# Rows that carry their expert's number, and activations in smaller steps

## The chip, the core and the metric

The kernel runs on one core of a Trainium2 chip. The core has a matrix engine (TensorE, PE in the trace), three engines for other arithmetic (VectorE = DVE, ScalarE = ACT, GpSimd = POOL), a queue engine (SyncE = SP) and 16 DMA engines. Each engine works through its own instructions in order; semaphores tie them together. The metric is the device time of one execution in microseconds, the median of several runs.

## The reference

One decoder block over 256 tokens of 1024 numbers: modulation by a conditioning vector (adaLN), two attention branches with gates, and an expert layer of 128 x 128 experts. The expert layer is the part that the change touches:

```python
q = (ht @ w_pq).reshape(T, PEER_HEADS, 2, PEER_HALF)          # 256 tokens, 8 heads
sub = jnp.einsum('thpc,hpnc->thpn', q, peer_keys)             # scores of 128 keys, twice a head
s_top, i_top = lax.top_k(sub, 16)
cand_s = s_top[:, :, 0, :, None] + s_top[:, :, 1, None, :]    # 16 x 16 sums
best_s, pos = lax.top_k(cand_s.reshape(T, 8, 256), 16)
expert = jnp.take_along_axis(cand_i, pos, axis=-1)            # 128 experts for each token
gate = jax.nn.softmax(best_s, axis=-1)
act = jax.nn.gelu(jnp.einsum('cd,ckd->ck', xc, peer_u[expert]))
out = jnp.einsum('ck,ckd->cd', gate * act, peer_v[expert])
```

## The kernel before

It computes the expert layer densely: every expert's activation for all 256 tokens, times a weight that is zero where the token did not choose the expert. Experts stand in 128 row blocks of 128: block `j` holds the experts 128 p + j, p being the partition. One block of `u` is a load of 512 KB on SP, a copy to a high half on ACT, the rest as a low half by a subtraction (`split`, L94) on DVE or GpSimd, and 24 matmuls on PE (eight chunks, three each: high x high, high x low, low x high). Blocks go in pairs; a pair ends in gelu on ACT and 256 KB of activations.

The stages in order, with the function that stands for each:

- attention, merge, and the query projection (`proj` of `w_pq`). The first five sixths of the adaLN rows come as `background` work in the attention (`ada`, two rows of 512 KB a time, called by `bg`), the last eight in the query projection (`ada_one`).
- search: for each half of the tokens, four groups of scores, each with `top16` on DVE, then the sums, `top16` again, and the selection: comparisons and products over 128x2048 bf16 (`eq`) on DVE, softmax, transposes on PE.
- grid: 64 steps of four tokens. DVE writes one-hot tables `E`, `A` and twice `B`, PE multiplies them (`grid_mm`, 16 matmuls), ACT copies the product to `G`, the weights of all blocks.
- ranking: from a count `used`, each of the 120 x 128 experts of blocks 0 to 119 is classed (first half of the tokens, both, second half, none) and gets a place `at_i`.
- put: the row of 256 weighted activations of each expert goes by an indirect DMA (scatter, issued on POOL) to its place in `w_rows` in memory. Blocks that were done before `G` was there had their activations spilled to `act_spill`; `put_rows` loads them back into one of four buffers `w`, DVE multiplies by `G`, POOL scatters. Blocks done after that are scattered straight from the tile `as`. Beside it, `sort_some` builds the inverse list, from place to expert, with one-hot tables `R`, `C`, `N` and 120 matmuls into `listed`; the end of it is the list `expert`.
- last stage: `w_rows` is read in order of the places, class by class; rows of one class need only one half of the tokens. Blocks 120 to 127 (`d`) take no places. For each 128 places the rows of `v` are gathered by an indirect DMA with the indices `expert[:, c]`, split, and multiplied into four accumulators.

What sets the order: the program is written out in one order, and each engine gets its instructions nearly in that order; a load is issued as soon as its buffer is free. How many blocks of `u` go beside the search and the grid is set by shares: `u_some(share)` collects shares and issues a whole pair, 48 matmuls, when they reach one. `PACE_R` and `PACE_G` divide the shares of the search and of the grid. Low halves are made by GpSimd (`split_by`) until the places are known, and by DVE from then on. Everything waits in order on its engine, so a multiplication that waits for its load holds the splits behind it.

Of the kernel before, what the change touches and what calls it, by code (L numbers as in the profile page):

```python
# [11 lines left out]
I32 = mybir.dt.int32  # L12
# [20 lines left out]
PACE_R = 3.8  # L33
PACE_G = 5.0
# [5 lines left out]
def kernel(  # L40
# [39 lines left out]
    w_rows = dpool.tile([NQ * P, T], F32, name="w_rows")  # L80
# [124 lines left out]
    background = [lambda t=t: ada(t) for t in range(16, 40, 2)]  # L205
# [384 lines left out]
    def upair(j, name):  # L590
        ps = pp.tile([P, 2, T], F32, tag="pp", name=f"pu{name}")
        for s in range(2):
            hi, lo = unit(u[j + s], f"u{j + s}")
            for k in range(NC8):
                mm3(ps[:, s], hi[:, k], lo[:, k], hh[:, k], hl[:, k], k == 0, k == NC8 - 1)
        return ps

    def u_spill(j):
        a = upool.tile([P, 2, T], F32, tag="a", bufs=2, name=f"as{j}")
        after, low[0] = low[0], split_by[0]  # L600
        nc.scalar.activation(a, upair(j, f"s{j}"), AF.Gelu_apprx_tanh)  # L601
        low[0] = after
        if places:
            nc.vector.tensor_mul(a, a, Gs[0][:, j : j + 2] if j < NQ else Gs[1][:, j - NQ : j - NQ + 2])  # L604
        if places and j < NQ:
            for s in range(2):
                put_row(a[:, s], j + s)
        else:
            nc.scalar.dma_start(act_spill[j // 2], a.rearrange("p a t -> p (a t)"))


    places, Gs, scatters = [], [], []
# [81 lines left out]
    for tt in range(2):  # L694
# [3 lines left out]
        for q in range(4):  # L698
# [169 lines left out]
    rc_i = npool.tile([P, 2, P], I32, name="rc_i")  # L868
    nc.vector.tensor_scalar(rc_i[:, 0], at_i, P - 1, None, op0=OP.bitwise_and)
    nc.vector.tensor_scalar(rc_i[:, 1], at_i, 7, None, op0=OP.logical_shift_right)  # L870
    rc = qpool.tile([P, 2, P], BF16, name="rc")
    nc.vector.tensor_copy(rc, rc_i)
    col = qpool.tile([P, P], BF16, name="col")
    nc.vector.tensor_copy(col, iota4[:, :, 0])
# [9 lines left out]
    listed = pn.tile([P, 2, NQ], F32, tag="n", name="listed")  # L884
    places.append(at_i)
    split_by[0] = nc.vector
    first_put = spilled[0]

    def sort_some(b):

        j4 = slice(4 * b, 4 * b + 4)
        R = spool.tile([P, P, 4], BF16, tag="R", name=f"R{b}")
        C = spool.tile([P, 2, NQ, 2], BF16, tag="C", name=f"C{b}")
        N = spool.tile([P, 2, 2, NQ, 2], BF16, tag="N", name=f"N{b}")
        pairs = lambda x: x[:, j4].rearrange("p (h i) -> p h i", h=2)[:, :, None, :].to_broadcast([P, 2, NQ, 2])
        nc.vector.tensor_tensor(R, rc[:, 0, None, j4].to_broadcast([P, P, 4]), iota4, op=OP.is_equal)
        nc.vector.tensor_tensor(
            C, pairs(rc[:, 1]), iota4[:, None, 0:NQ, 0:2].to_broadcast([P, 2, NQ, 2]), op=OP.is_equal
        )
        nc.scalar.activation(N[:, :, 0], C, AF.Copy, scale=row)  # L900
        nc.vector.tensor_tensor(N[:, :, 1], C, pairs(col), op=OP.mult)
        for i in range(4):
            j = 4 * b + i
            nc.tensor.matmul(listed, R[:, :, i], N[:, i // 2, :, :, i % 2], start=(j == 0), stop=(j == NQ - 1))
# [19 lines left out]
    for j in puts:  # L924
        put_rows(j)
# [235 lines left out]
```

## Time and profile before

| | us |
|---|---|
| median of 3 runs | 1123.38 (1122.06 to 1124.8) |
| profiled execution | 1127.95 |
| its span | 1126.2 |
| busy in the span: PE, DVE, ACT, POOL | 1007.6, 815.6, 556.0, 436.6 |

The span is the time between the first and the last instruction of the core; the profiled execution's own time is 1.75 us longer. "Busy" is the time in which an engine has an instruction in work; issuing a DMA from a queue is not counted, but POOL's work for an indirect DMA is. Matmuls are pipelined, so that the mean time of one in the trace is longer than the distance from one to the next.

### The profile page before, as it was taken

What the parts mean: (1) busy time and instruction counts of PE and PEld (TensorE: products, weight loads), DVE (VectorE), ACT (ScalarE), POOL (GpSimd) and SP (SyncE); (2) the same over time, 40 slices, a digit from 0 to 9 for tenths busy, and PEclk for the clock granted to TensorE, in tenths of its full rate; (3) what the DMA queues carried; (4) which work ended last, traced back from release to release, by engine and by line L of the source; (5) the groups of instructions that cost most, each with busy time, mean ns of one, the idle gap of its engine ahead of it and who ended that gap; (6) DMA issues with size and microseconds to landing.
All of it is one profiled execution on the core that took longest, in us unless ns stands there. A gap on an engine that the chain in (4) does not pass through costs nothing. (4 is left out here: it accounts for less than half of the span.)

```text
span 1126.2 us, 19893 instructions
## 1 busy us (share of the span) xinstructions
PE 1007.6 (89%) x7540; PEld 925.1 (82%) x7543; DVE 815.6 (72%) x1589; ACT 556.0 (49%) x779; POOL 436.6 (39%) x293
## 2 busy tenths in 40 slices
PE   7889999989989796888888988777999899999995
PEld 4879989988989696878888987766999688888884
DVE  7788877775579999888777565556764577767765
ACT  4495345654455354444444533333553466656652
POOL 0000000000186677333333377776644065666540
PEclk9999999998999898999999999998999999999998
DMA  9964575346764455233222577777867799999981
GB/s 344 368 237 148 183 256 212 132 154 235 270 216 169 159 187 189 67 108 109 94 94 95 191 241 248 253 255 263 265 216 269 271 306 307 312 317 303 324 282 39
DMA packets 90826, 244.65 MB, mean 217 GB/s; under 512 B 10977, under 2 KB 33121, under 8 KB 90594
## 3 DMA queue, kind: packets, MB, share of 16 engines
q1 hardware_dynamic: 63794, 162.24, 42.9%
q0 software_dynamic: 20592, 69.74, 17.3%
q10 hardware_dynamic: 6336, 11.31, 2.7%
q8 instruction: 61, 1.00, 0.4%
q14 instruction: 43, 0.35, 0.1%
HBM read 215.20 MB, written 28.05 MB: 216 GB/s over the span
## 5 line engine op out<-in xcount | busy, mean ns | idle before, releaser
L96 POOL TENSOR_TENSOR l_u<-r_u,h_u 128x1024 fp32r<-128x1024 f32 x66 | 170.3, 2595 | 457.4 <-ACT h_u L95 457.4
L101 PE MATMUL pus<-hh_n,l_u 128*128 128x256 f32 x1024 | 297.9, 291 | 25.6 <-DVE l_u L96 25.5
L99 PE MATMUL pus<-hh_n,h_u 128*128 128x256 f32 x1024 | 299.7, 293 | 1.0 <-ACT as L601 1.0
L100 PE MATMUL pus<-hl_n,h_u 128*128 128x256 f32 x1024 | 295.1, 288 | 0.0
L95 ACT ACTIVATE h_u<-r_u 128x1024 fp32r<-128x1024 f32 x128 | 135.5, 1060 | 224.7 <-DMA r_u<-in_u_dram 108.4
L101 PEld LDWEIGHTS pus<-hh_n,l_u 128*128 128x128 f32 x1024 | 201.1, 196 | 30.0 <-DVE l_u L96 29.9
L99 PEld LDWEIGHTS pus<-hh_n,h_u 128*128 128x128 f32 x1024 | 201.6, 197 | 1.4 <-ACT as L601 1.2
L100 PEld LDWEIGHTS pus<-hl_n,h_u 128*128 128x128 f32 x1024 | 200.9, 196 | 0.0
L96 DVE TENSOR_TENSOR l_v<-r_v,h_v 128x1024 fp32r<-128x1024 f32 x111 | 133.7, 1224 | 46.8 <-ACT h_v L95 42.8
L978 POOL DMA_INDIRECT r_v<-in_v_dram,expert x103 | 122.0, 1184 | 115.5 <-DVE l_v L96 90.4
L95 ACT ACTIVATE h_v<-r_v 128x1024 fp32r<-128x1024 f32 x111 | 116.7, 1054 | 45.6 <-PE acc L101 36.8
L818 DVE TENSOR_TENSOR B<-E,selT 128x768 bf16<-128x768 bf16 x128 | 96.1, 783 | 31.7 <-PE used L801 30.4
L615 POOL DMA_INDIRECT w_rows<-w,at_i x66 | 80.5, 1219 | 37.3 <-ACT N L900 11.3
L797 PE MATMUL pg<-B,A 128*128 128x128 bf16 x768 | 70.5, 228 | 26.2 <-DVE B L818 19.8
L96 DVE TENSOR_TENSOR l_u<-r_u,h_u 128x1024 fp32r<-128x1024 f32 x62 | 75.8, 1223 | 24.3 <-ACT h_u L95 24.1
L797 PEld LDWEIGHTS <-A 128*128 128x128 bf16 x768 | 61.2, 116 | 32.3 <-issue 20.7
L615 POOL DMA_INDIRECT w_rows<-as,at_i x54 | 63.7, 1179 | 45.5 <-DVE as L604 33.6
L100 PE MATMUL acc<-l_v,whb 128*128 128x512 f32 x200 | 78.7, 394 | 2.5 <-DVE l_v L96 2.5
L99 PE MATMUL acc<-h_v,whb 128*128 128x512 f32 x200 | 78.2, 392 | 0.5 <-PEq L1020 0.5
L101 PE MATMUL acc<-h_v,wlb 128*128 128x512 f32 x200 | 78.5, 393 | 0.1
L911 DVE TENSOR_TENSOR w<-w,G 128x256 f32<-128x256 f32 x66 | 27.9, 427 | 62.0 <-DMA w<-act_spill 61.6
L805 ACT ACTIVATE G<-pg 128x480 f32<-128x480 f32 x64 | 36.5, 570 | 62.6 <-PE pg L797 58.8
(370 smaller groups left out, 2338.3 us busy)
## 6 DMA issues: line engine op xcount, KB each, us to landing
r_u<-in_u_dram SPq DMA_DIRECT2D x128, 512.0 KB, 3.7
ada<-in_w_ada_dram SPq DMA_DIRECT2D x20, 1024.0 KB, 7.7
act_spill<-as ACTq DMA_DIRECT2D x37, 256.0 KB, 3.3
w<-act_spill SPq DMA_DIRECT2D x66, 128.0 KB, 3.1
r_g<-in_w_in_dram SPq DMA_DIRECT2D x16, 512.0 KB, 3.9
r_pq<-in_w_pq_dram SPq DMA_DIRECT2D x16, 512.0 KB, 5.8
ab<-w_rows SPq DMA_DIRECT2D x25, 256.0 KB, 5.9
r_first<-in_w_in_dram SPq DMA_DIRECT2D x8, 512.0 KB, 7.1
```

The source lines that it names most:

```text
L95: nc.scalar.activation(hi, src, AF.Copy)
L96: last_split[:] = [low[0].tensor_sub(lo, src, hi.bitcast(F32))]
L99: nc.tensor.matmul(ps, lh, rh, start=start, stop=False)
L100: nc.tensor.matmul(ps, lh, rl, start=False, stop=False)
L101: nc.tensor.matmul(ps, ll, rh, start=False, stop=stop)
L615: o = nc.gpsimd.indirect_dma_start(out=w_rows, out_offset=bass.IndirectOffsetOnAxis(ap=places[0][:, j : j + 1], axis=0), in_=w, in_offset= ...
L797: nc.tensor.matmul(ps[:, t], A[:, :, t], Bs[t // 2][:, x, :, t % 2], start=(x == 0), stop=(x == 2))
L805: nc.scalar.activation(g[:, :, 4 * b : 4 * b + 4], ps[:, :, q].rearrange("p t j -> p j t"), AF.Copy)
L818: nc.vector.tensor_tensor(B, E[:, None, :, 2 * q : 2 * q + 2].to_broadcast([P, 3, P, 2]), g, op=OP.mult)
L911: nc.vector.tensor_mul(w, w, G[:, j + s])
L978: nc.gpsimd.indirect_dma_start(out=raw, out_offset=None, in_=v, in_offset=bass.IndirectOffsetOnAxis(ap=expert[:, c : c + 1], axis=0))
```

## The change

- **The number in the row.** `w_rows` has 257 columns (`ROW`) instead of 256. Between the two halves of the tokens, at column 128, stands the number of the row's expert, 128 p + j, written by ACT into the tile before the scatter. So `sort_some`, `listed` and `expert` go. Tiles that are scattered get a gap: 128 columns, the number, 128 columns; the load from the spill is cut into two pieces of 128 columns. In the last stage the weights' load brings the number along (rows of one half: 129 columns, from one side or the other), and the gather of `v` takes its index from that tile.
- **Steps.** `u_steps` is a generator that gives the work on `u` in steps of one chunk, three matmuls; 16 steps are a pair. The load and split of a block are issued two blocks ahead of its matmuls.
- **Shares.** `PACE_R` 3.8 becomes 3.2 and `PACE_G` 5.0 becomes 3.3; one more pair goes before the transposes of each selection.
- **Splits.** GpSimd makes low halves only from the first group of scores up to the third of each half of the tokens; DVE makes the rest.
- **adaLN.** All rows come in the attention, four more pairs by `bg(2)`; `ada_one` goes.
- **Buffers.** `w` eight instead of four, loaded weights four instead of three, their halves four instead of two, and weights are loaded three items ahead instead of two.

```diff
-PACE_R = 3.8
-PACE_G = 5.0
+PACE_R = 3.2
+PACE_G = 3.3
+ROW = T + 1
-    background = [lambda t=t: ada(t) for t in range(16, 40, 2)]
+    background = [lambda t=t: ada(t) for t in range(16, 48, 2)]
...
-            bg()
+            bg(2)
...
+    def u_done(j, ps):
+        a = upool.tile([P, 2, ROW + 1], F32, tag="a", bufs=2, name=f"as{j}")
+        if places and j < NQ:
+            ah = a.rearrange("p s (h n) -> p s h n", h=2)[:, :, :, 0:P]
+            th = lambda x: x.rearrange("p s (h t) -> p s h t", h=2)
+            nc.scalar.activation(ah, th(ps), AF.Gelu_apprx_tanh)
+            nc.vector.tensor_mul(ah, ah, th(Gs[0][:, j : j + 2]))
+            nc.scalar.activation(a[:, :, P : P + 1].bitcast(I32), numbers[0][:, j : j + 2, None], AF.Copy)
+            for s in range(2):
+                put_row(a[:, s, 0:ROW], j + s)
...
+        make(0)
+        make(1)
+        for j in range(0, NJ, 2):
+            ps = pp.tile([P, 2, T], F32, tag="pp", name=f"pu{j}")
+            for s in range(2):
+                if j + s + 2 < NJ:
+                    make(j + s + 2)
+                hi, lo = ready.pop(0)
+                for k in range(NC8):
+                    mm3(ps[:, s], hi[:, k], lo[:, k], hh[:, k], hl[:, k], k == 0, k == NC8 - 1)
+                    if s == 0 or k < NC8 - 1:
+                        yield
+            u_done(j, ps)
+            done[0] = j + 2
+            yield
...
     def u_some(share):
-        spilled[1] += share
-        while spilled[1] >= 1.0 and spilled[0] < NJ:
-            u_spill(spilled[0])
-            spilled[0] += 2
-            spilled[1] -= 1.0
+        owed[0] += 2 * NC8 * share
+        while owed[0] >= 1.0:
+            owed[0] -= 1.0
+            next(steps, None)
...
-            for t in range(32 + 2 * b, 34 + 2 * b) if b >= 4 else ():
-                ada_one(t)
...
+            split_by[0] = nc.gpsimd if q < 3 else nc.vector
             u_some(4.0 / PACE_R)
...
+        u_some(1.0)
         ps = pr_.tile([P, 3, P], F32, tag="t", name=f"psel{tt}")
...
-            w = spool.tile([P, T], F32, tag="w", bufs=4, name=f"w{j + s}")
-            nc.sync.dma_start(w, act_spill[j // 2][:, T * s : T * s + T])
-            nc.vector.tensor_mul(w, w, G[:, j + s])
-            put_row(w, j + s)
+            w = spool.tile([P, ROW + 1], F32, tag="w", bufs=8, name=f"w{j + s}")
+            wh = w.rearrange("p (h n) -> p h n", h=2)[:, :, 0:P]
+            th = lambda x: x.rearrange("p (h t) -> p h t", h=2)
+            nc.sync.dma_start(wh, th(act_spill[j // 2][:, T * s : T * s + T]))
+            nc.vector.tensor_mul(wh, wh, th(G[:, j + s]))
+            nc.scalar.activation(w[:, P : P + 1].bitcast(I32), number[:, j + s : j + s + 1], AF.Copy)
+            put_row(w[:, 0:ROW], j + s)
...
+    for i in range(2 * left):
+        u_some(0.5)
+        while puts and n_puts - len(puts) < n_puts * (i + 1) / max(1, 2 * left - 6):
             put_rows(puts.pop(0))
...
-            out=raw, out_offset=None, in_=v, in_offset=bass.IndirectOffsetOnAxis(ap=expert[:, c : c + 1], axis=0)
+            out=raw, out_offset=None, in_=v, in_offset=bass.IndirectOffsetOnAxis(ap=no, axis=0)
```

How this moves instructions shows at three places. The first is DVE in the middle of the grid; `l_u` is a low half of `u`. Before:

```order
L811 TENSOR_TENSOR E_6816<-selT,iota_2860 128x512
L818 TENSOR_TENSOR B_0_6820<-E_6816,selT 128x768
L818 TENSOR_TENSOR B_1_6822<-E_6816,selT 128x768
L811 TENSOR_TENSOR A_6844<-selT,iota_2860 128x512
L811 TENSOR_TENSOR E_6843<-selT,iota_2860 128x512
```

And after:

```order
L830 TENSOR_TENSOR E_6943<-selT,iota_2888 128x512
L837 TENSOR_TENSOR B_0_6947<-E_6943,selT 128x768
L98 TENSOR_TENSOR l_u_6937<-r_u_6934,h_u_6936 128x1024
L830 TENSOR_TENSOR A_6944<-selT,iota_2888 128x512
L837 TENSOR_TENSOR B_1_6949<-E_6943,selT 128x768
```

The low halves, which stood on POOL in the grid, now stand between the one-hot tables on DVE.

The second is DVE in the put stage; `w` are the reloaded blocks, `as` a pair that is put straight. Before:

```order
L911 TENSOR_TENSOR w_8841<-w_8841,G 128x256
L911 TENSOR_TENSOR w_8845<-w_8845,G 128x256
L896 TENSOR_TENSOR R_8590<-rc,iota_2860 128x512
L901 TENSOR_TENSOR N_8592<-C_8591,col 128x2x240
L96 TENSOR_TENSOR l_u_8551<-r_u_8548,h_u_8550 128x1024
L604 TENSOR_TENSOR as_8346<-as_8346,G 128x512
L897 TENSOR_TENSOR C_8761<-rc,iota_2860 128x480
L911 TENSOR_TENSOR w_8849<-w_8849,G 128x256
```

And after:

```order
L98 TENSOR_TENSOR l_u_8963<-r_u_8960,h_u_8962 128x1024
L605 TENSOR_TENSOR as_8933<-as_8933,G 128x4x128
L909 TENSOR_TENSOR w_9036<-w_9036,G 128x2x128
L909 TENSOR_TENSOR w_9041<-w_9041,G 128x2x128
L98 TENSOR_TENSOR l_u_9003<-r_u_9000,h_u_9002 128x1024
L909 TENSOR_TENSOR w_9046<-w_9046,G 128x2x128
L909 TENSOR_TENSOR w_9051<-w_9051,G 128x2x128
L909 TENSOR_TENSOR w_9087<-w_9087,G 128x2x128
```

The one-hot tables are gone, and between two pairs of `u` stand about six multiplications of reloaded blocks instead of four.

The third is POOL where the put stage ends. Before, the gathers of `v` take their indices from the list:

```order
L615 DMA w_rows<-w_10235,at_i 15360x256
L615 DMA w_rows<-as_9215,at_i 15360x256 x2
L978 DMA r_v_10681<-in_v_dram,expert 128x1024
L978 DMA r_v_10687<-in_v_dram,expert 128x1024
L978 DMA r_v_10711<-in_v_dram,expert 128x1024
```

And after, from the loaded weights `a` (one half of the tokens) and `ab` (both):

```order
L591 DMA w_rows<-w_10086,at_i 15360x257
L976 DMA r_v_10482<-in_v_dram,a_10365 128x1024
L976 DMA r_v_10488<-in_v_dram,a_10365 128x1024
L976 DMA r_v_10512<-in_v_dram,a_10407 128x1024
L976 DMA r_v_10518<-in_v_dram,a_10407 128x1024
L976 DMA r_v_10542<-in_v_dram,ab_10449 128x1024
```

Each gather now stands behind the load of its own weights, and the last scatters are those of reloaded blocks, no longer of direct ones.

## Rows read from the trace of the kernel before

**Rows 1.** Busy time by stretch: from:to, length, busy (instructions) per engine, clock, DMA.

```profile
core 0: us, PE busy (x) PEld busy (x) DVE busy (x) ACT busy (x) POOL busy (x), PEclk, DMA share, GB/s
307.00:450.00 143.00, 120.39 (x955) 118.48 (x955) 129.58 (x465) 70.44 (x81) 102.73 (x40) 0.92 0.54 185
450.00:620.00 170.00, 143.75 (x1603) 137.69 (x1603) 135.68 (x250) 71.25 (x163) 60.52 (x24) 0.96 0.28 94
620.00:639.00 19.00, 19.00 (x167) 18.89 (x167) 9.75 (x29) 9.01 (x13) 4.85 (x2) 1.00 0.51 173
639.00:793.00 154.00, 121.97 (x925) 116.36 (x925) 91.91 (x172) 56.20 (x72) 111.12 (x96) 0.94 0.76 249
793.00:874.00 81.00, 80.65 (x673) 79.93 (x672) 51.31 (x71) 39.72 (x50) 39.94 (x30) 1.00 0.77 257
...
924.00:1092.00 168.00, 168.00 (x743) 139.12 (x742) 119.90 (x127) 105.98 (x127) 99.01 (x84) 1.00 0.91 310
```

**Rows 2.** Waits of PE: waited for what, us in total, times, longest.

```profile
PE pus L101 <- DVE l_u L96: 25.5, 20, 3.4
PE pg L797 <- DVE B L818: 19.8, 12, 1.8
PE psel L769 <- DVE sel L758: 16.7, 2, 9.0
```

**Rows 3.** Tiles eq and B (min/median/max ns), and GpSimd's splits (busy us, mean ns).

```profile
L754 DVE TENSOR_TENSOR eq<-rb,ranks x4: 1209/3434/3446, 355.2 to 433.2; 128x2048 bf16<-128x2048 bf16 x4
L755 DVE TENSOR_TENSOR eq<-eq,at x4: 3370/3445/3449, 356.5 to 439.4; 128x2048 bf16<-128x2048 bf16 x4
...
L818 DVE TENSOR_TENSOR B<-E,selT x128: 546/556/2789, 386.4 to 617.3; 128x768 bf16<-128x768 bf16 x128
...
L96 POOL TENSOR_TENSOR l_u<-r_u,h_u 128x1024 fp32r<-128x1024 f32 x66 | 170.3, 2595 | 457.4 <-ACT h_u L95 457.4
```

**Rows 4.** One grid step on DVE, then on PE: start us, length us, instruction.

```profile
480.74 0.42 DVE L811 TENSOR_TENSOR A<-selT,iota 128x512 bf16<-128x512 bf16 x1
...
481.53 1.03 DVE L818 TENSOR_TENSOR B<-E,selT 128x768 bf16<-128x768 bf16 x2
482.47 0.42 DVE L811 TENSOR_TENSOR A<-selT,iota 128x512 bf16<-128x512 bf16 x1
...
480.41 0.37 PE L797 MATMUL pg<-B,A 128*128 128x128 bf16 x3 [0.35 <-ACT Gd L805]
...
481.36 0.36 PE L101 MATMUL pus<-hh_n,l_u 128*128 128x256 f32 x1
```

**Rows 5.** Groups of instructions: busy us, mean ns, idle time before and its releaser.

```profile
L615 POOL DMA_INDIRECT w_rows<-as,at_i x54 | 63.7, 1179 | 45.5 <-DVE as L604 33.6
...
L911 DVE TENSOR_TENSOR w<-w,G 128x256 f32<-128x256 f32 x66 | 27.9, 427 | 62.0 <-DMA w<-act_spill 61.6
```

**Rows 6.** Scatters on POOL in order of time, and a split on DVE beside one.

```profile
707.49 0.96 POOL L615 DMA_INDIRECT w_rows<-as,at_i  x1 [0.30 <-DVE C L897]
...
847.99 1.89 POOL L615 DMA_INDIRECT w_rows<-as,at_i  x1 [0.31 <-issue]
...
847.82 1.23 DVE L96 TENSOR_TENSOR l_u<-r_u,h_u 128x1024 fp32r<-128x1024 f32 x1 [1.36 <-ACT h_u L95]
```

**Rows 7.** The tile w_rows (min/median/max ns, first and last start), and the gathers.

```profile
L615 POOL DMA_INDIRECT w_rows<-w,at_i x66: 955/962/2024, 639.4 to 795.3; - x66
L615 POOL DMA_INDIRECT w_rows<-as,at_i x54: 954/960/2012, 650.3 to 854.1; - x54
...
L978 POOL DMA_INDIRECT r_v<-in_v_dram,expert x103 | 122.0, 1184 | 115.5 <-DVE l_v L96 90.4
```

**Rows 8.** DMA queues and times to landing, 672 to 784 us; last, 924 to 1090.

```profile
q1 hardware_dynamic: 10536, 19.12, 55.5%
q0 software_dynamic: 3408, 9.31, 21.4%
...
w<-act_spill SPq DMA_DIRECT2D x49, 128.0 KB, 3.3
w_rows<-w,at_i POOLq DMA_INDIRECT x48, 4.1
...
q1 hardware_dynamic: 11296, 8.06, 16.4%
```

More of the change, by code (lines that the diff above doesn't have):

```diff
@@ L588 @@
     raws.append(ctx.enter_context(tc.tile_pool(name="raw_u", bufs=3, side="right")))
[L590 to L612, printed above, removed]
+    places, numbers, Gs, scatters = [], [], [], []
     def put_row(w, j):
@@ L867 @@
     nc.vector.tensor_copy(at_i, at[:, 0])
[L868 to L874, printed above, removed]
     over = npool.tile([1, 4], F32, name="over")
@@ L883 @@
     spool = es_s.enter_context(tc.tile_pool(name="sorted", bufs=2, side="right"))
-    listed = pn.tile([P, 2, NQ], F32, tag="n", name="listed")
+    number = qpool.tile([P, P], F32, name="number")
+    nc.vector.tensor_scalar(number, iota4[:, :, 0], row, None, op0=OP.add)
     places.append(at_i)
[L886 to L904, printed above, removed]
@@ L906, in put_rows @@
+    numbers.append(number)
+    first_put = done[0]
     def put_rows(j):
         for s in range(2):
-            w = spool.tile([P, T], F32, tag="w", bufs=4, name=f"w{j + s}")
-            nc.sync.dma_start(w, act_spill[j // 2][:, T * s : T * s + T])
-            nc.vector.tensor_mul(w, w, G[:, j + s])
-            put_row(w, j + s)
-    lists, puts = list(range(NQ // 4)), list(range(0, first_put, 2))
-    n_lists, n_puts = len(lists), len(puts)
-    left = (NJ - spilled[0]) // 2
-    for i in range(left):
-        u_some(1.0)
-        share = (i + 1) / max(1, left - 3)
-        while puts and n_puts - len(puts) < n_puts * share:
+            w = spool.tile([P, ROW + 1], F32, tag="w", bufs=8, name=f"w{j + s}")
[5 more added lines that the diff above has]
+            put_row(w[:, 0:ROW], j + s)
@@ L921 @@
+    puts = list(range(0, first_put, 2))
+    n_puts = len(puts)
+    left = (NJ - first_put) // 2
+    for i in range(2 * left):
+        u_some(0.5)
+        while puts and n_puts - len(puts) < n_puts * (i + 1) / max(1, 2 * left - 6):
             put_rows(puts.pop(0))
-        while lists and n_lists - len(lists) < n_lists * share:
-            sort_some(lists.pop(0))
-    for j in puts:
-        put_rows(j)
+    u_some(NJ)
     es_G.close()
-    expert = kpool.tile([P, NQ], I32, name="expert")
@@ L955, in weights @@
         k, t = len(cs), T if wide else P
[L956 to L957 removed]
+        a = (pool or apl).tile([P, 2, ROW + 1], F32, tag="a", name=f"a{nm}")
+        hl = [(split_pool or wpool).tile([P, 2 * T], F32R, tag=x, name=f"{x}{nm}") for x in ("wh", "wl")]
+        no = []
         if kind == "d":
+            aw = a.rearrange("p s r -> p (s r)")[:, 0 : 2 * T]
             nc.sync.dma_start(aw, act_spill[cs[0] // 2])
+            split(hl[0], hl[1], aw)
         else:
[L961 removed]
+            n_ = ROW if wide else P + 1
+            c0 = 0 if wide else P * kind
             o = nc.sync.dma_start(
[L963 to L964 removed]
+                a[:, 0:k, 0:n_], w_rows[P * cs[0] : P * cs[0] + P * k, c0 : c0 + n_].rearrange("(s p) r -> p s r", p=P)
             )
@@ L967, in weights, with v_unit @@
                 tc.add_manual_dep(o.ins, i.name, data_dep)
-        hl = [(split_pool or wpool).tile([P, 2 * T], F32R, tag=x, name=f"{x}{nm}") for x in ("wh", "wl")]
-        split(hl[0][:, 0 : k * t], hl[1][:, 0 : k * t], aw)
+            no = [a[:, s, P - c0 : P - c0 + 1].bitcast(I32) for s in range(k)]
+            if wide:
+                x = [y[:, 0 : k * t].rearrange("p (s h t) -> p s h t", s=k, h=2) for y in hl]
+                split(x[0], x[1], a[:, 0:k].rearrange("p s (h n) -> p s h n", h=2)[:, :, :, 0:P])
+            else:
+                x = [y[:, 0 : k * t].rearrange("p (s t) -> p s t", s=k) for y in hl]
+                split(x[0], x[1], a[:, 0:k, kind : kind + P])
         at_ = lambda s, tt: slice(s * t + (P * tt if wide else 0), s * t + (P * tt if wide else 0) + P)
-        return hl, at_, (0, 1) if wide else (kind,)
-    def v_unit(kind, c):
+        return hl, at_, (0, 1) if wide else (kind,), no
+    def v_unit(kind, c, no):
         if kind == "d":
@@ L991 @@
     n_items = len(items)
-    ahead = [weights(0), weights(1)]
+    ahead = [weights(i) for i in range(3)]
     todo = []
@@ L997 @@
             raws.append(ctx.enter_context(tc.tile_pool(name="raw_v", bufs=6)))
-        vs = [v_unit(kind, c) for c in cs]
-        if n + 2 < n_items:
-            ahead.append(weights(n + 2))
+        vs = [v_unit(kind, c, w[3][s] if w[3] else None) for s, c in enumerate(cs)]
+        if n + 3 < n_items:
+            ahead.append(weights(n + 3))
         if n == n_items - 3:
```

42 lines of the change are left out of this document (22 added, 20 removed).

## The prediction

> **What bounds the kernel now.** I read the busy time by stretch first, with stretches cut where the work changes [rows 1]. From 924 us on, PE is busy for all of 168 us and nothing else matters there. Free PE time lies earlier: 22.6 us in the search (307 to 450), 26 in the grid (450 to 620), 32 in the first part of the scatters (639 to 793). The granted clock is below 1 in just these three. A row block of `u` is 24 matmuls; in 793 to 874, where PE waits for nothing, one matmul takes 80.65 / 673 = 0.120 us, so a block costs 2.88 us. Any saving must come from laying blocks into the gaps.
>
> Next, the waits of PE [rows 2]: for the low halves that DVE makes, for B of the grid, for the end of the selection. All three point at DVE, so I read what holds DVE. Its bf16 operations are the tell: the comparison over 2048 elements takes 1.209 us once and 3.4 the other times, B takes 0.556 at the median and up to 2.789, and the splits on GpSimd run at the same time, 2.6 us each [rows 3]. DVE stands still until the GpSimd split ends. Without that it makes the grid's four operations in 482.47 - 480.74 = 1.73 us [rows 4].
>
> In the scatters it is a ring of four buffers: 66 multiplications by G take 0.43 us each but had 62 us of idle time before them, waiting for their loads [rows 5], and a load waits for a scatter to give its buffer back. POOL itself is close behind: the least scatter is 0.96 us, with 0.30 between two in a row [rows 6]. 120 scatters run from 639.4 to 854.1 [rows 7], 1.80 us apiece, and in the dense part 96 in 154 us [rows 1], 1.60.
>
> **The change part by part.** The profiled execution took 1127.95 us (span 1126.2 and 1.75 around it), 4.6 over the median 1123.38; I make the sum against the former and carry the difference to the median.
>
> *Search.* Per half of the tokens the shares sum to 34.6: before 34.6 / 3.8, now 34.6 / 3.2 plus 1, so 47.25 blocks in both halves instead of 36.4. PE: 955 + 10.8 x 24 = 1215 matmuls x 0.120 = 146 us, and some 5 us of the 16.7 at the two ends of selection, as a pair of 5.8 us now stands ahead of the transposes: 151. DVE: 129.6 busy; the two kinds of 2048-wide operation fall from 3.4 to 1.2 for seven of eight (the selection is now free of GpSimd), less 15.6; 30 of the blocks are split on DVE instead of GpSimd, 30 x 1.22 = 36.9: also 151. Both at the edge: I take 153, **+10**. Ends: 146 (+3); 166 where no stall is given back (+23).
>
> *Grid.* 64 / 3.3 = 19.4 pairs, 0.606 blocks a step instead of 0.4. PE: 16 small matmuls 481.36 - 480.41 = 0.95 us [rows 4] plus 0.606 x 2.88 = 1.75, 64 steps: 172.5 us. DVE: 1.73 + 0.606 x 1.22 = 2.47, 158 us, hidden beside PE. The 19.8 us for B go with GpSimd's splits. I take 178, **+8**; ends 172.5 (+2) and 198, all of today's 26 us of idle time kept (+28). That matmuls come in groups of three, and not 48 at once, is what lets PE take B as it comes; I price it only in that nearness to the lower end.
>
> *Ranking,* 620 to 639: two pairs as before, the same chain: 0. The bits and casts that go took under 2 us there, beside PE.
>
> *Scatters.* 43 pairs are done after the grid, two more in the ranking, so 90 blocks are put from spills and 30 straight, and 19 pairs are left instead of 31. PE then has 19 x 5.76 = 109 us of work, and the 120 scatters set the pace. R, C, N and `listed` go (30 x 3 on DVE, 30 on ACT, 120 on PE, the last only where PE waits anyway). A number is added to each row: 105 ACT operations of one or two columns. ACT is busy 56 of 154 us [rows 1], so it hides anything up to 0.9 us apiece; the scatter waits for it, but for DVE's multiplication as well. The ring has eight buffers, and a round is 3.3 us for the load, 0.4 on DVE, a turn on POOL and 4.1 to land [rows 8], some 10 us: 1.3 us a buffer, and only three scatters of four use one. What is left is POOL. A scatter that starts beside the f32 split at 847.82 takes 1.89 and not 0.96: it waits for that split's end as well [rows 6]. The nearest row without bf16 work on DVE is the gather, 1.184 us mean [rows 7]; with 0.30 between, 1.48 x 120 = 178. Behind the last of them part of the three pairs that follow, 10 us: 188 instead of 235, **-47**. Ends: 0.96 + 0.30, 159 (-76); today's 1.80, 226 (-9).
>
> The Trainium skill (SBUF — State Buffer, "SBUF: two separate sides") calls the pair of ports that DVE and GpSimd share a lock that one holds for a whole instruction, and in its warning on GpSimd's transfers names only DVE's two-port modes. By the warning alone, f32 splits would hold up no scatter and the pace would be the lower end, 159 us; the row at 847.99 contradicts it here, and agrees with the lock as the section has it for two inputs in SBUF.
>
> *Rows with a number.* The gather of `v` waits for its weights' load, where the list let gathers run ahead of the last blocks. In the steady part, loads are issued three items ahead and POOL waits for raw buffers, so 0. At the hand-over four items without a number (8 blocks, some 21 us) stand against load, gather and split of the first: twice 4.1 to land as the scatters do [rows 8], 1.2 on POOL and a split of 1.2 on DVE, 11 us, more when the queues are full. Behind a late gather stand all later ones on POOL. **+3**, ends 0 and +8.
>
> *adaLN.* Eight dot products of 1.22 us and 4 MB of loads go from the query projection to the attention; PE is full in both, DVE has a quarter free: 0, +-3.
>
> Sum: 10 + 8 - 47 + 3 = -26: 1102 in the profile, 1097 in the median.
>
> **The rivals.**
> *A, the forecast,* POOL sets the pace of the scatters: 1097, itself 1082 to 1113.
> *B, more is hidden.* DVE is busy 60% now [rows 1], less when scatters spread over fewer splits. At 1.30 us a scatter the stretch is 166 (-69); search and grid at +5 and +5: 1067. Against it: a direct put waits for DVE's multiplication after gelu, and POOL sat idle 33.6 us for that before 54 puts [rows 5].
> *C, DVE takes the front.* 49 splits move to it net, 60 us. If nothing comes back from the stalls and search and grid end near their upper ends (+23, +22), with -47 and +3: 1124, no change. For it: DVE has 129.6 of 143 us busy. Against it: rows 3.
> *D, slower: the odd row.* A row is 1,028 bytes, no row begins where a power of two does, and the spills are loaded in halves of 512 bytes. In 672 to 784 queue 0 took 21.4% for 71 scatters, 0.34 us of all engines each, and queue 1 55.5% for 24 blocks and 49 loads [rows 8]; a block at 310 GB/s in a 0.91 share [rows 1] is 1.54, so a load is 0.51. A pair with 7.6 scatters needs 3.1 + 2.9 + 2.6 = 8.5 us, 1.12 a scatter, under POOL's pace. If scatters and loads cost double, 1.84: 120 x 1.84 + 10 = 231 (-4). The last stage, 0.91 with 16.4% in the loads of weights [rows 8], would pass 1: 168 x 1.07 = +12. With +18 in front and +3: 1152. It decides from 1.70 a scatter, where -21 no longer pays for the front. Rows with such starts do not occur in the trace, so nothing excludes it and nothing speaks for it; the engines' time per row must grow by half before it binds, hence a small chance.
>
> The Trainium skill (DMA: Bandwidth & Descriptors, "How a descriptor splits into AXI transactions") has a piece that starts off a 256-byte boundary fetch from the boundary below: on average 126 bytes more on 1,028, an estimate of 12% from that page, and no run here shows it; by that, D would stay under POOL's pace.
>
> **How the numbers follow.** A 0.47, B 0.23, C 0.14, D 0.12, 0.04 for what I do not see. A measurement tells about 0.2%, 2.2 us, from no change. A and B are faster; C spreads around none, 0.06 faster, 0.05 the same, 0.03 slower; D and the rest slower but for 0.01 each: faster 0.77, same 0.06, slower 0.17. The range takes in A, most of B and C's middle: 1066 to 1127.
>
> **What would show it.** Right: the search at 150 to 156 us with the 2048-wide operations at 1.2 in both halves and DVE over 90% busy; the grid at 175 to 182 with PE over 93% busy and no B over 0.6; scatters of 1.1 to 1.25 us with 0.3 between, 175 to 185 us from first to last, DVE's wait for loads gone, PE half idle and at a lower clock there; from 20 us behind the last block of `u` PE full. Wrong: long B or `eq` beside nothing on POOL (C), queue shares near 1 with scatters waiting for free queue slots (D), or POOL idle for the direct puts or for ACT's numbers, which would put the pace where it is today.

## The result and the profile after

The changed kernel takes 1086.31 us (median of 3 runs, 1085.0 to 1092.15) against 1123.38: ratio 0.9683, 95% interval 0.9626 to 0.9741. The forecast was 1097. The profiled execution took 1085.0 us with a span of 1083.2, 43.0 less than the span before; the forecast sum was -26. Some 6 of the 43 lie in which executions were profiled (before 4.6 us above its median, now 1.3 below); the medians are 37 us apart.

Busy time by stretch of the changed kernel, cut where the work changes (columns as in [rows 1]):

```profile
258.00:304.00 46.00, 43.36 (x358) 42.72 (x357) 17.19 (x16) 21.18 (x27) 6.03 (x3) 1.00 0.67 222
304.00:451.00 147.00, 145.91 (x1218) 145.37 (x1218) 127.69 (x495) 83.16 (x94) 35.40 (x15) 1.00 0.64 210
451.00:456.00 5.00, 2.94 (x28) 2.84 (x28) 2.40 (x5) 1.44 (x2) 0.00 (x0) 1.00 0.81 279
456.00:629.00 173.00, 173.00 (x1924) 170.33 (x1922) 153.42 (x286) 89.65 (x183) 0.00 (x0) 1.00 0.43 146
629.00:645.00 16.00, 16.00 (x144) 15.89 (x142) 9.71 (x25) 8.48 (x19) 0.00 (x0) 1.00 0.67 213
645.00:816.00 171.00, 121.62 (x799) 115.32 (x798) 82.89 (x137) 56.54 (x148) 131.22 (x120) 0.85 0.83 258
...
880.00:1048.00 168.00, 168.00 (x721) 135.16 (x721) 118.75 (x124) 104.46 (x125) 100.53 (x83) 1.00 0.92 309
```

From the query projection's end to the first scatter, 307 to 639, it was 332 us [rows 1]; it is 341 now, and PE is busy in all but 3 of them, at a granted clock of 1.00. The 120 scatters took 214.7 us from first to last start [rows 7] and now take 170.1, with PE idle for 49 of 171 us. From the last scatter to the end it was 272.1 us and is 267.8. The query projection is 3 us shorter. -3 + 8.9 - 44.6 - 4.3 = -43.0.

That DVE no longer stands still shows in the tiles `eq`, `B` (min/median/max ns, first and last start), the rows that answer to [rows 3]:

```profile
L772 DVE TENSOR_TENSOR eq<-rb,ranks x4: 1210/1218/1228, 355.9 to 437.4; 128x2048 bf16<-128x2048 bf16 x4
L773 DVE TENSOR_TENSOR eq<-eq,at x4: 1210/1217/1218, 358.2 to 438.7; 128x2048 bf16<-128x2048 bf16 x4
```
```profile
L837 DVE TENSOR_TENSOR B<-E,selT x128: 546/553/1569, 386.7 to 625.1; 128x768 bf16<-128x768 bf16 x128
```

The B of 1.57 us lies in the search, where GpSimd still makes some splits; in the grid the longest is 0.561 us.

In the scatters GpSimd works nearly without a break. Its groups in that stretch (busy us, mean ns, idle time before and its releasers; the 247.7 lie before the first scatter) answer to [rows 5, 7]:

```profile
L591 POOL DMA_INDIRECT w_rows<-w,at_i x90 | 100.8, 1120 | 271.3 <-ACT w L910 247.7 <-issue 18.6 <-DVE w L909 2.2
L591 POOL DMA_INDIRECT w_rows<-as,at_i x30 | 31.6, 1055 | 12.3 <-issue 5.2 <-DVE as L605 4.1 <-DMA w_rows<-w,at_i 1.2
```

That is 132.4 us of work, and 170.1 / 119 = 1.43 us from one start to the next. Between two scatters stand 0.30 us even where the engine waits for nothing ("issue"). POOL's waits between 650 and 810 us (us in all, times, longest) show that it waited for little else:

```profile
POOL w_rows L591 <- issue: 22.9, 75, 0.3
POOL w_rows L591 <- DVE as L605: 4.1, 3, 1.8
POOL w_rows L591 <- ACT w L910: 3.7, 12, 0.3
POOL w_rows L591 <- DVE w L909: 3.1, 10, 0.4
```

The short ones are the same 0.3 us under another name. Read one by one, 116 of the 119 gaps are 0.36 us or less; the other three, 4.1 us in all, are waits for a straight pair's multiplication. The scatters themselves are 0.96 us at the least and together 17 us over that. Of the 39 that take more than 1.0 us, 34 end 0.82 to 0.85 us after a DVE operation over f32 that was running when they began, as in [rows 6]:

```profile
674.03 1.22 DVE L98 TENSOR_TENSOR l_u<-r_u,h_u 128x1024 fp32r<-128x1024 f32 x1
674.25 1.83 POOL L591 DMA_INDIRECT w_rows<-w,at_i  x1 [0.30 <-issue]
```

So scatters and the 0.30 us between them fill all but some 3 of the 172 us: GpSimd sets the pace. The other engines wait as well. What PE, DVE, ACT and SyncE's queue waited for in the same window:

```profile
PE pu L101 <- ACT as L604: 18.4, 6, 7.0
PE pu L101 <- ACT h_u L97: 17.7, 8, 6.1
PE pu L103 <- DVE l_u L98: 13.2, 14, 2.5
```
```profile
DVE w L909 <- DMA w<-act_spill: 60.0, 48, 4.4
```
```profile
ACT w L910 <- DMA w_rows<-w,at_i: 73.8, 48, 8.0
```
```profile
SPq L908 <- DMA w_rows<-w,at_i: 100.6, 47, 6.9
```

In the last row SyncE stands before 47 reloads until a scatter has landed and given its buffer back. By itself that does not make the ring a second bound: ahead of an engine that is never free, all buffers are full and loads wait for them. The times to landing in 672 to 784 us (last number, us) are longer than in [rows 8]:

```profile
q0 software_dynamic: 3839, 10.53, 24.6%
...
r_u<-in_u_dram SPq DMA_DIRECT2D x21, 512.0 KB, 6.0
w<-act_spill SPq DMA_DIRECT2D x58, 128.0 KB, 4.6
w_rows<-w,at_i POOLq DMA_INDIRECT x58, 5.4
```

The theory that the runs put to the test is **T**, the forecast's: GpSimd's 1.43 us a scatter is the pace. Its rivals are named with the runs: the list (L), the odd rows (D), the transfers and the loop from a landed scatter to the next reload (M, Q), a queue blocked by the writing of numbers (N).

### The profile page after: what moved, and what is told of

It is laid out like the page before. It is cut to its first block, busy times and chain, and to the rows that moved or that the text cites. A ratio compares the mean times of both kernels' runs of the same rounds, so it can differ in the third digit from the quotient of the medians.

```text
span 1083.2 us, 19804 instructions
## 1 busy us (share of the span) xinstructions
PE 994.5 (92%) x7423; PEld 910.7 (84%) x7423; DVE 778.7 (72%) x1552; ACT 554.1 (51%) x853; POOL 300.1 (28%) x244
## 5 line engine op out<-in xcount | busy, mean ns | idle before, releaser
L101 PE MATMUL pu<-hh_n,h_u 128*128 128x256 f32 x1024 | 305.8, 299 | 36.5 <-ACT as L604 18.4
L103 PE MATMUL pu<-hh_n,l_u 128*128 128x256 f32 x1024 | 299.4, 292 | 13.2 <-DVE l_u L98 13.2
L102 PE MATMUL pu<-hl_n,h_u 128*128 128x256 f32 x1024 | 297.5, 291 | 0.0
L101 PEld LDWEIGHTS pu<-hh_n,h_u 128*128 128x128 f32 x1024 | 204.6, 200 | 39.8 <-ACT h_u L97 19.6
L103 PEld LDWEIGHTS pu<-hh_n,l_u 128*128 128x128 f32 x1024 | 204.4, 200 | 16.4 <-DVE l_u L98 16.4
L102 PEld LDWEIGHTS pu<-hl_n,h_u 128*128 128x128 f32 x1024 | 204.7, 200 | 0.0
L591 POOL DMA_INDIRECT w_rows<-w,at_i x90 | 100.8, 1120 | 271.3 <-ACT w L910 247.7
L98 DVE TENSOR_TENSOR l_u<-r_u,h_u 128x1024 fp32r<-128x1024 f32 x111 | 135.3, 1221 | 36.4 <-ACT h_u L97 35.4
L98 POOL TENSOR_TENSOR l_u<-r_u,h_u 128x1024 fp32r<-128x1024 f32 x17 | 41.4, 2442 | 359.3 <-ACT h_u L97 359.3
L976 POOL DMA_INDIRECT r_v<-in_v_dram,a x53 | 65.5, 1235 | 63.8 <-DMA a<-w_rows 34.6
L976 POOL DMA_INDIRECT r_v<-in_v_dram,ab x50 | 60.6, 1211 | 47.9 <-DMA ab<-w_rows 17.6
```

The lines of the kernel that those rows point to most:

```text
L98: last_split[:] = [low[0].tensor_sub(lo, src, hi.bitcast(F32))]
L101: nc.tensor.matmul(ps, lh, rh, start=start, stop=False)
L102: nc.tensor.matmul(ps, lh, rl, start=False, stop=False)
L103: nc.tensor.matmul(ps, ll, rh, start=False, stop=stop)
L591: o = nc.gpsimd.indirect_dma_start(out=w_rows, out_offset=bass.IndirectOffsetOnAxis(ap=places[0][:, j : j + 1], axis=0), in_=w, in_offset= ...
L976: nc.gpsimd.indirect_dma_start(out=raw, out_offset=None, in_=v, in_offset=bass.IndirectOffsetOnAxis(ap=no, axis=0))
```

## Experiments

The times are medians; the ratio is to the kernel before on the same chip; the marks are the first and last start of a scatter and the end of the span in the profiled execution, us. Differences in the text are of medians; where they are small, the ratios are the better guide, since the runs did not all share a chip.

| kernel | us | ratio, 95% | first | last | end | scatters | rest |
|---|---|---|---|---|---|---|---|
| before | 1123.38 | | 639.4 | 854.1 | 1126.2 | 214.7 | 272.1 |
| changed | 1086.31 | 0.9683 (0.9626 to 0.9741) | 645.3 | 815.4 | 1083.2 | 170.1 | 267.8 |
| 1 ring of four | 1127.23 | 1.0014 (0.9985 to 1.0043) | 648.1 | 873.5 | 1128.0 | 225.4 | 254.5 |
| 2 list, ring of four | 1110.83 | 0.9859 (0.9802 to 0.9916) | 648.9 | 858.3 | 1111.4 | 209.4 | 253.1 |
| 3 GpSimd splits | 1129.61 | 1.0047 (1.0024 to 1.0070) | 689.3 | 857.3 | 1124.1 | 168.0 | 266.8 |
| 4 old shares | 1075.20 | 0.9549 (0.9509 to 0.9590) | 604.6 | 807.3 | 1074.6 | 202.7 | 267.3 |
| 5 half plain | 1083.47 | 0.9636 (0.9608 to 0.9664) | 646.0 | 811.2 | 1080.8 | 165.2 | 269.6 |
| 6 spread | 1090.36 | 0.9675 (0.9641 to 0.9710) | 602.6 | 824.0 | 1088.6 | 221.4 | 264.6 |
| 7 spread, three pairs | 1087.50 | 0.9678 (0.9616 to 0.9739) | 602.4 | 821.9 | 1087.5 | 219.5 | 265.6 |
| 8 adaLN late | 1089.83 | 0.9682 (0.9663 to 0.9702) | 651.0 | 823.4 | 1090.2 | 172.4 | 266.8 |
| 9 number on DVE, ring of four | 1149.04 | 1.0187 (1.0122 to 1.0253) | 649.8 | 896.1 | 1150.0 | 246.3 | 253.9 |
| 10 number on DVE | 1097.74 | 0.9742 (0.9713 to 0.9771) | 646.0 | 831.9 | 1103.7 | 185.9 | 271.8 |
| 11 old shares, number on DVE | 1085.40 | 0.9622 (0.9586 to 0.9659) | 600.7 | 816.9 | 1084.9 | 216.2 | 268.0 |
| 12 spread, writes behind | 1095.22 | 0.9720 (0.9684 to 0.9756) | 601.9 | 828.3 | 1095.0 | 226.4 | 266.7 |

**1, the ring.**

```diff
-            w = spool.tile([P, ROW + 1], F32, tag="w", bufs=8, name=f"w{j + s}")
+            w = spool.tile([P, ROW + 1], F32, tag="w", bufs=4, name=f"w{j + s}")
```

> The ring of reloaded blocks has four buffers instead of eight, all else as in the changed kernel. T (GpSimd's pace sets the put stage, and the ring of eight is what lets it): in the kernel before, 66 reloaded blocks took 156 us through four buffers, 2.36 us each, a round of 9.4 us; 90 blocks then take 212 us or more, so the put stage is 220 to 250 us instead of 183 and the time 1120 to 1155 us, with GpSimd idle between scatters and DVE waiting for loads. Rival L (the removed list is the gain, the ring is not): within 5 us of the changed kernel, 1081 to 1091.

1127.23: the whole gain is gone, and 225 us of scatters are inside T's 220 to 250. Now GpSimd waits for reloaded blocks (650 to 810 us):

```profile
POOL w_rows L591 <- DVE w L909: 21.2, 15, 4.8
```

Four buffers pass a block every 225.4 / 90 = 2.50 us, a round of 10.0 us. Its parts add up to that: 3.9 us for the load, 0.4 on DVE, 1.1 on POOL, 4.6 to land. With eight the parts are 4.6, 0.4, 1.1 and 5.4, so 11.5, and the round is 170.1 / 90 x 8 = 15.1: there the ring has room to spare. (Both sums are estimates from median landings and mean times.)

**2, the list** in place of the number, and the ring of four. By my count its tables and a ring of eight do not fit into the memory together, so that no run has both; that the removed list pays as room rests on this count.

```diff
+        nc.vector.tensor_tensor(R, rc[:, 0, None, j4].to_broadcast([P, P, 4]), iota4, op=OP.is_equal)
...
+            nc.tensor.matmul(listed, R[:, :, i], N[:, i // 2, :, :, i % 2], start=(j == 0), stop=(j == NQ - 1))
...
-            nc.scalar.activation(w[:, P : P + 1].bitcast(I32), number[:, j + s : j + s + 1], AF.Copy)
```

> The inverse list with its comparisons and 120 matmuls back in place of the number in each row (rows of 1,024 bytes, gathers fed by the list), with a ring of four, since list and ring of eight do not fit into the memory together; compared with the run with the number and a ring of four. T: within 6 us of that run, since DVE's 90 and TensorE's 120 further operations lie where both wait for the ring; gathers run ahead again, -3 us. Rival L: slower than that run by 20 us or more. Rival D (odd rows of 1,028 bytes cost transfer time): faster than that run by 10 us or more.

16 us faster than number with ring of four. L falls: with four buffers the list cost less than the number that replaces it. (What the list cost by itself is not shown; PE waited 28.2 us before its matmuls between 650 and 810 us.) T's 6 us were too few, and D's line was met. Times to landing with the list, then with the number, 672 to 784 us:

```profile
w<-act_spill SPq DMA_DIRECT2D x46, 128.0 KB, 3.4
w_rows<-w,at_i POOLq DMA_INDIRECT x48, 3.7
```
```profile
w<-act_spill SPq DMA_DIRECT2D x43, 128.0 KB, 3.9
w_rows<-w,at_i POOLq DMA_INDIRECT x43, 4.6
```

Longer landings (D) could make it, or the new writes on ScalarE, which waited 109.5 us there for the ring (N, experiments 9 to 12). D is large enough: by its parts the list's round is 3.4 + 0.4 + 1.2 + 3.7 = 8.7 us, 1.3 less, where the rounds measured differ by 0.7 (209.4 / 90 x 4 = 9.3). No run takes D away alone. By these two runs the change's gain comes apart into steps: front and finer steps with list and ring of four -13.8 (1124.61 to 1110.83), number for list +16.4, ring of eight -40.9 (-37 by the ratios).

**3, GpSimd's splits.**

```diff
-            split_by[0] = nc.gpsimd if q < 3 else nc.vector
...
+    split_by[0] = nc.vector
     first_put = done[0]
```

> GpSimd makes the low halves of u until the places are known, as in the kernel before; all else as in the changed kernel. T with S (the blocks fit into search and grid only because DVE no longer stands still beside GpSimd's splits): comparisons of 2048 elements at 3.4 us in place of 1.21 in seven of eight, B up to 2.8 us, and 2.6 us for each split on GpSimd with 2.9 us of matmuls per block: search and grid together 15 to 35 us longer, 1100 to 1120 us, put stage unchanged at 183. Rival (DVE is the bound in the front, 87% busy in the search): DVE is relieved of some 55 splits of 1.2 us and the time falls, to 1060 to 1080.

43.3 us slower, all of it ahead of the first scatter (44.0 later), the scatters as long as before. The stalls are back, in the tile `eq`, in the mean of `B` (990 ns in the grid; under it the row of the changed kernel, 562) and in PE's waits in search and grid:

```profile
L772 DVE TENSOR_TENSOR eq<-eq,at x4: 1210/3420/3424, 359.2 to 442.3; 128x2048 bf16<-128x2048 bf16 x4
```
```profile
L836 DVE TENSOR_TENSOR B<-E,selT 128x768 bf16<-128x768 bf16 x124 | 122.7, 990 | 7.7 <-PE used L819 1.5
L837 DVE TENSOR_TENSOR B<-E,selT 128x768 bf16<-128x768 bf16 x128 | 70.4, 562 | 8.1 <-PE used L820 4.8
```
```profile
PE pg L815 <- DVE A L829: 18.3, 26, 1.4
```

The direction is T's, the size is above its 35. GpSimd makes 88 splits in search and grid here and made some 64 before, since more blocks lie in the front; that this is the excess is argued.

**4, the shares.**

```diff
-PACE_R = 3.2
-PACE_G = 3.3
+PACE_R = 3.8
+PACE_G = 5.0
```

> The shares of u's blocks beside search and grid as before (3.8 and 5.0 in place of 3.2 and 3.3), all else as in the changed kernel. T: TensorE is full in the front (146 of 147 us and 173 of 173), so some 24 blocks of 2.9 us fewer give 25 to 45 us back there; the put stage then has some 31 pairs of 5.8 us, 180 us, about as long as 120 scatters of 1.43 us, and ends at 195 to 205 us instead of 183: 1055 to 1075 us. Rival F (moving blocks forward is itself the gain, as TensorE's time in the put stage decides): the put stage returns to 215 to 235 us and the time is 1090 to 1110.

1075.20, faster than both kernels: the front gives back 40.7 us, the scatters take 32.6 more. The time is 0.2 us over T's 1055 to 1075, but the way there was partly missed: from the first scatter to the last block of `u` it is 217 us (605 to 822), not T's 195 to 205 and inside F's 215 to 235. F's time is refuted: blocks moved forward were no gain in themselves. Its scatter stretch, dense part and rest:

```profile
604.00:738.00 134.00, 102.47 (x708) 99.63 (x708) 67.95 (x110) 46.36 (x118) 103.35 (x95) 0.87 0.86 269
738.00:807.00 69.00, 67.25 (x548) 67.05 (x548) 34.97 (x36) 30.20 (x45) 27.20 (x25) 0.98 0.72 226
```

The 70 reloaded blocks go in the first row, the last of them at its end, at 1.41 us a scatter; in the second PE is nearly full and GpSimd waits for its pairs.

**5, half of the rows without GpSimd.** This kernel leaves the sorting by class out; the bytes are the same.

```diff
     def put_row(w, j):
+        if j % 2:
+            o = nc.scalar.dma_start(w_rows[P * j : P * j + P], w)
...
+    nc.vector.tensor_scalar(at_i, iota4[:, :, 0], float(P), own, op0=OP.mult, op1=OP.add)
```

> The changed kernel, in which the 60 odd rows of blocks go out by plain transfers that ScalarE issues, to places 128 x block + partition, and the other 60 stay GpSimd's scatters, to places by the same rule; this leaves the sorting by class out, with the bytes moved the same. T (GpSimd's pace of 1.43 us a scatter sets the put stage): GpSimd needs 60 x 1.43 = 86 us, TensorE's 19 pairs 109, and the transfers (0.83 of 171 us) 142, which is next: the stage falls from 183 to 145 to 160 us, the time to 1048 to 1065 us. Rival M (the transfers set the pace, by their landing or the loads of the ring): the stage stays at 175 to 185 and the time within 8 us of the changed kernel.

GpSimd's work halves, and the scatters take 165.2 us in place of 170.1. T's forecast of 145 to 160 us for the stage fails and M's holds: 182 us (646 to 828), and a time that is not clear of the changed kernel's. The stretch, its queues in 672 to 784 us:

```profile
645.00:700.00 55.00, 39.60 (x284) 38.18 (x282) 26.02 (x47) 17.48 (x52) 22.32 (x20) 0.87 0.95 259
700.00:760.00 60.00, 41.68 (x266) 39.19 (x266) 28.32 (x47) 19.26 (x53) 25.60 (x22) 0.83 0.93 251
760.00:816.00 56.00, 40.09 (x263) 37.67 (x264) 27.65 (x45) 18.76 (x45) 22.05 (x19) 0.85 0.99 269
```
```profile
q1 hardware_dynamic: 18833, 18.61, 65.6%
q10 hardware_dynamic: 5886, 5.39, 16.5%
q0 software_dynamic: 1922, 5.29, 15.6%
```

GpSimd is busy 70 of 171 us, the transfers 0.93 to 0.99 (0.83 before this edit): the next bound lies only some 5 us under GpSimd's. In the changed kernel itself GpSimd decides, by its own waits above. What the next bound is, this run settles only in part. The transfers are nearly full, but ScalarE now issues half of them and PE waited 26.0 us for its gelu; and a plain row took more of the queues, 16.5% of 112 us / 40 = 0.46 us, than a scatter there, 15.6% / 42 = 0.42, or one in the changed kernel, 24.6% / 80 = 0.34.

**6 and 7, the order on GpSimd.** Experiment 4 with the reloads held behind the scatter ahead of them, and with a third buffer for a pair.

```diff
-            put_rows(puts.pop(0))
+            with tc.issue_after(scatters[-1]) if scatters else ExitStack():
+                put_rows(puts.pop(0))
```

> The run with the old shares, and reloaded blocks held behind the last straight scatter that stands ahead of them, so that GpSimd has two or three of them between two pairs to the end in place of five at first and none later. T: with the old shares the 120 scatters took 203 us, 95 in the first 134 (1.41 each) and 25 in the last 69, where they came at TensorE's pace; spread, they go back to back to the end, 120 x 1.43 = 172 us, beside 25 pairs of 5.8 us: 25 to 32 us less, 1043 to 1052 us. Rival O (TensorE's wait for gelu, 33 us there, comes from the two buffers of pairs and not from the order on GpSimd): the waits stay and the time is 1068 to 1078 us.

> As the run with spread scatters, and three buffers in place of two for a pair of u on its way to the scatters. T: GpSimd's queue is the bound and a deeper buffer only lengthens the queue ahead of it: within 5 us of the run with two. Rival O: TensorE's wait for gelu goes with the third buffer, 15 us or more faster than with two.

15.2 us slower than experiment 4, not 25 faster; the third buffer gives 2.9, within the intervals. In experiment 7 GpSimd is busy 126 of 218 us, some 160 with 0.30 behind each scatter, so it is no longer what sets the length. O is right that PE's waits for gelu stay, but its 1068 to 1078 was missed too, and a third buffer doesn't take the waits away. In experiment 7, 603 to 820 us, PE, ACT and SyncE's queue:

```profile
PE pu L101 <- ACT as L604: 37.5, 19, 5.8
```
```profile
ACT w L910 <- DMA w_rows<-w,at_i: 119.2, 55, 6.2
```
```profile
SPq L908 <- DMA w_rows<-w,at_i: 99.0, 46, 5.6
```

**8, adaLN** as before in the query projection.

```diff
-    background = [lambda t=t: ada(t) for t in range(16, 48, 2)]
+    background = [lambda t=t: ada(t) for t in range(16, 40, 2)]
...
+            for t in range(32 + 2 * b, 34 + 2 * b) if b >= 4 else ():
+                ada_one(t)
```

> The changed kernel, with the last eight dot products of adaLN back in the second half of the query projection, as before. T: the query projection takes 49 us again in place of 46, and nothing else moves: 0 to 5 us slower, 1086 to 1091 us. Rival (they cost the attention as much as the projection gained): 0 to 3 us faster, 1083 to 1086 us.

3.5 us by the medians, but the ratios are the same (0.9682 and 0.9683): not settled by the time. In the profile the search's first matmul starts at 306.6 in place of 304.4, the 2 us that the move was worth there.

**9 to 11, the number of a reloaded block on DVE.**

```diff
-            nc.scalar.activation(w[:, P : P + 1].bitcast(I32), number[:, j + s : j + s + 1], AF.Copy)
+            nc.vector.tensor_copy(w[:, P : P + 1].bitcast(I32), number[:, j + s : j + s + 1])
```

> The run with a ring of four, and the number of a reloaded row written by DVE right behind its multiplication, not by ScalarE. Two theories for the 16 us by which list and ring of four were faster than number and ring of four. N (the write on ScalarE waits for the scatter that still holds the buffer, and gelu and the high halves of u queue behind it): the 16 us come back, 1108 to 1116 us. D (rows of 1,028 bytes and loads in halves of 512 bytes take longer, 3.9 and 4.6 us to land in place of 3.4 and 3.7, and the ring's round with them): 1123 to 1130 us.

> The changed kernel with the number of a reloaded row written by DVE. ScalarE waited 73.8 us there for scatters that held the buffer, and TensorE 18.4 us for gelu and 17.7 for high halves. T (GpSimd sets the put stage, full for 158 of 171 us): within 4 us of the changed kernel, 1082 to 1090. N: TensorE's waits for ScalarE go, and what GpSimd leaves open with them: 8 to 20 us faster, 1066 to 1078.

> The run with the old shares, and the number of a reloaded row written by DVE. TensorE waited 33.3 us for gelu in its put stage of 203 us, ScalarE 52.5 for the ring and 52.0 for the buffers of pairs. N: the stage ends 15 to 30 us earlier, 1045 to 1060 us. T: in the first 134 us GpSimd is full with 95 scatters and the write has no part in it: 1070 to 1080 us.

All three are slower by the medians, by 22, 11 and 10 us, and by 19, 7 and 8 by the ratios; only the first is clear of the intervals, and experiment 10's marks come from an execution 8 us over its median. None of the forecast times came, since "right behind its multiplication" was wrong: the write needs only the buffer, so the order put it up to a round of the ring ahead of the load. In experiment 9, 650 to 810 us, DVE and PE; then the same two places with the write on ScalarE (experiment 1):

```profile
DVE w L910 <- DMA w_rows<-w,at_i: 78.3, 30, 5.8
```
```profile
PE pu L103 <- DVE l_u L98: 47.2, 13, 4.8
```
```profile
ACT w L910 <- DMA w_rows<-w,at_i: 109.5, 44, 7.0
```
```profile
PE pu L101 <- ACT as L604: 44.4, 13, 6.7
```

The early write stops whichever engine holds it, and PE then waits for that engine. That much of N is shown. In the changed kernel the write on ScalarE can cost the scatters little, since GpSimd waited for others some 4 us in all; what it costs the 12 us of `u` behind the last scatter is not shown.

**12, both writes behind work of the same row,** on experiment 7.

```diff
+            with tc.issue_after(gelu.ins):
+                nc.scalar.activation(a[:, :, P : P + 1].bitcast(I32), numbers[0][:, j : j + 2, None], AF.Copy)
...
+            with tc.issue_after(made.ins):
+                nc.vector.tensor_copy(w[:, P : P + 1].bitcast(I32), number[:, j + s : j + s + 1])
```

> The run with spread scatters and three buffers of pairs, with both writes of numbers put where their engine has already waited: that of a reloaded row on DVE behind the row's multiplication, that of a pair on ScalarE behind its gelu. N (a write of a number that stands ahead of its row's other work stops its in-order engine until a scatter has landed): ScalarE's wait of 119 us for the ring goes, TensorE's 37.5 us for gelu fall under 10, and the scatters take 172 to 190 us from first to last in place of 220: 1040 to 1063 us, against 1087.5. Rival Q (SyncE's queue is what stops: it waited 97.5 us for landed scatters, with the loads of u behind in the same queue): ScalarE's wait goes but TensorE then waits for loads of u and for DVE's low halves, and the time is 1078 to 1095 us.

1095.22, 0.2 over Q's upper end; PE's wait for gelu goes (2.5 us) and the scatters still take 226 us, so N falls as the cause of that stage's length. The 119 us of ScalarE did not go, they changed their name (PE, ACT, SyncE's queue, 603 to 820 us):

```profile
PE pu L103 <- DVE l_u L98: 28.3, 13, 5.7
```
```profile
ACT h_u L97 <- DMA r_u<-in_u_dram: 118.7, 41, 7.4
```
```profile
SPq L909 <- DMA w_rows<-w,at_i: 61.7, 31, 6.6
SPq L107 <- DVE l_u L98: 30.0, 15, 4.2
```

Loads of `u` and reloads stand in one queue in order; a reload that waits for a landed scatter holds the loads of `u` behind it, which fits these rows. With reloads spread to the end (6, 7, 12) this lasts for the whole stage; in experiment 4 it ends at 738 us, and PE is nearly full from there. That this sets the length of the stage is argued: a queue of their own for the loads of `u` would test it directly, and was not tried.

## Why the prediction was right, and where it was not

- *Size and direction* hold: 1086 in a likeliest case's range of 1082 to 1113. The sum was -26 and came out at -43. Of the 17 us, 5 lie in the grid, 5 in the scatters, 3 each in ranking and adaLN, 1 in the search, all on the same side.
- *Search and grid:* forecast +10 and +8, measured with the hand-over between them +9 and +3. Both mechanisms were as forecast: all eight long comparisons at 1.21 to 1.23 us, no B over 0.6 in the grid, PE full, DVE at 127.7 of 147 rather than over 90%. Experiment 3 shows that the freed DVE pays for the front, 43 us. I took values above the lower end for nearness to DVE's limit, and PE alone set the time; C's condition did not come.
- *Ranking and adaLN:* 0 each forecast, -3 each measured. In the ranking PE has 144 instructions in place of 167, about one block of `u` less.
- *Scatters:* 188 us to the last stage forecast, 183 measured (645 to 828); 1.48 us a scatter forecast, 1.43 measured. "What is left is POOL" holds, and so does its price: 0.96 us, more beside DVE's f32 work, and 0.30 between two. The size of the extra time was taken from another kind of instruction, the gathers' 1.184 us; the scatters' mean was 1.12 and 1.06. PE was idle for 49 of 171 us, not for half. (The lower end of this term, 159, is 161 by its own working.)
- *The ring* was given a round of some 10 us. Its parts make 11.5, since landing grew from 4.1 to 5.4 us and the load's from 3.3 to 4.6; the slack was still there, as experiment 1 shows by taking it away. One sign failed: DVE's wait for loads did not go (60.0 us, 61.6 before [rows 5]). It was a wrong sign to name, since behind an engine that sets the pace the loads wait for buffers, and DVE for the loads.
- *What the prediction did not see* is how near the next limit lies: with half of GpSimd's work the scatters take only 5 us less (experiment 5). The prediction had the transfers at 1.12 us a scatter; by the DMA share it was 1.18 in the changed kernel (0.83 of 171 us for 120) and 1.36 in experiment 5, where half of the rows are plain.
- *Last stage:* +3 forecast, 252 to 255 measured, but not for the reason given. Gathers do wait for their weights' loads (35.5 and 18.5 us in POOL's waits), off PE's path: PE is idle for 15.0 us behind the last block of `u` and was for 16.1. That the number agrees is luck.
- *The shares.* I priced the front's growth and the scatters' gain as one change and did not ask whether the former was worth it. Experiment 4: it is not, 11 us are to be had by taking it back.
- *Rivals:* B's 1.30 us a scatter was not reached. D as worked out, doubled transfers, did not come: 24.6% for 80 scatters against 21.4% for 71 is 0.34 us each, as before, so that the estimate of 12% more does not show either; the weights' loads took 15.5% against 16.4%. But landings are longer with the number than with the list, and the 16 us between experiments 1 and 2 are not assigned.

## What to carry to other kernels

A removal can be worth more for the room it frees than for the work it saves: here number for list alone was 16 us slower, and the ring of eight, which by my count fits only without the list, was worth some 40 us. Whether an engine sets the pace is read from the gaps between its instructions, not from its busy share or from the waits of others: GpSimd was busy for 132 of 172 us and had three gaps over 0.36 us. Whether a ring sets it shows when the parts of its round are added up: 10.0 of 10.0 us with four buffers, 11.5 of 15.1 with eight. And the next limit can lie close behind: taking half the work off the engine gave 5 us. Look also at who stands in the same queue behind a load that waits. A small write that needs only a free buffer was put early in its engine's order here, and stopped the engine until that buffer's last transfer had landed.

## What the runs showed of the hardware

- A scatter on GpSimd takes 0.96 us alone, with 0.30 to the next. Beside a DVE operation over f32 it ends 0.83 us after that operation (34 of the 39 longer than 1.0 us).
- A plain transfer of 128 rows of 1,028 bytes took as much or more of the queues as a scatter of them (0.46 against 0.42 us of all engines in the same run, experiment 5), so taking rows off GpSimd did not take load off the transfers.
- Times to landing of the reloaded blocks' scatters, 672 to 784 us, grow with the DMA share: with rows of 1,028 bytes 4.6 us at 0.74 (experiment 1), 5.4 at 0.83 (changed), 7.1 at 0.98 (experiment 5). Load is not all of it: with rows of 1,024 bytes they were 3.7 and 4.1 us at 0.77 (experiment 2 and before).
- The granted clock averaged 0.85 of full speed in the scatters, where PE was busy for 122 of 171 us, and 0.79 with the ring of four (131 of 226). In the search and the grid, where PE had no gap to speak of, it was 1.00. In the kernel before it was below 1 not only in the three stretches that the prediction names, but also 0.97 in the query projection and 0.87 from 1092 us on.
